# The low part of the gate-and-up weights: by an accumulating transfer instead of a VectorE subtraction

## The chip, the core and the metric

One core of one Trainium2 chip runs the whole program in one launch. The metric is device time in microseconds, as the median of the runs that were made. Engines are named as in the profile: PE is TensorE (matrix products), DVE is VectorE, ACT is ScalarE, POOL is GpSimd, SP is SyncE, which issues transfers.

## The reference, cut to what matters

Two layers of a decoder trunk on 512 tokens of 1024 features, all in float32: a token mixer, a cross-attention into 256 memory tokens, and a feed-forward part. Each has a norm before it and one behind it, and adds to the residual stream. The change touches the feed-forward part alone:

```python
def swiglu_ffn(h, w_gate_up, w_down):
    gate, up = jnp.split(h @ w_gate_up, 2, axis=-1)
    return (jax.nn.silu(gate) * up) @ w_down
```

`w_gate_up` is 1024 x 5632 per layer (twice 2816 columns), `w_down` 2816 x 1024.

## The kernel before

**Products from two parts.** TensorE multiplies faster in the type fp32r, which keeps fewer bits of a float32. Each operand is therefore split into a high part (the value rounded to fp32r) and a low part (value minus high part), and a product is three products, `mm3` (L204 to L211): high by high, high by low, low by high. In the trace these are lines L207, L208 and L209. `split` (L213) does it with two instructions: ScalarE copies the source into the high part, and VectorE subtracts the high part from the source.

**Weights in chunks.** A weight matrix goes through in chunks of 512 KB: a tile of 128 partitions by 1024 columns. `load` (L241) lets SyncE fetch a chunk into a raw tile (three buffers, L158); for the gate-and-up weights it consists of four row blocks of 256 columns, so its rows in DRAM are 1 KB long. `chunk` (L256) splits it into the tiles `hi` and `lo` (five buffers each, L159). `load` is called three chunks ahead of the one in use and `chunk` makes two ahead, but that is the order in which the code is written down. The order in which each engine runs its instructions is set by a scheduler at compile time, which places a split as soon as its buffers allow by its estimate. All engines run their queues in order.

**The feed-forward part** (`ffn`, L1176). The hidden columns are handled in two parts of 12 and 10 blocks of 128. For each pair of blocks there is a group, named `gu` in the profile, of two gate blocks and two up blocks: four chunks, first two for the gate, then two for the up columns. A chunk serves 24 products. Gate blocks are evacuated from PSUM by ScalarE (`silu`), up blocks by VectorE (`silu` times up), and the result is split again (`gh`, `gl`). Behind each part follow products with `w_down`, named `da` and `db`. There are 11 groups per layer, 44 chunks of `gu`, 88 in both layers.

**The start of the part.** The norm ahead of it (`prenorm`, L361, names with `ff`) runs in four token blocks of 128, here called blocks 0 to 3, while TensorE finishes the output projection of the cross-attention (`xo0b` in layer 0, `xo1b` in layer 1) and begins with the first `gu` group. That group runs its four chunks twice: first for tokens 0 to 255, then for 256 to 511, so that it can begin before blocks 2 and 3 are normalised. The chain of one block is: ScalarE squares the projection (`junk`), VectorE prepares `xo0p_t`, GpSimd takes the power -0.5 (`xo0p_r`, L228), VectorE updates the residual `h`, ScalarE squares that (`ff_hn`), VectorE prepares `ff_t`, GpSimd takes the power (`ff_r`), VectorE writes the normalised `ff_hn`, TensorE transposes it (`ff_pt`), and ScalarE and VectorE split the transpose into `hTff_h` and `hTff_l`. The transposes of blocks 2 and 3 stand in TensorE's queue among the products of the first `gu` group.

GpSimd does little else than these powers; all transfers are issued by SyncE.

Of the kernel before, what the change touches and what calls it, by code (L numbers as in the profile page):

```python
# [10 lines left out]
F32 = mybir.dt.float32  # L11
F32R = mybir.dt.float32r
# [14 lines left out]
# SBUF tiles of 2 KB, by stream: slots of a stream are given out in the order of emission  # L27
# [6 lines left out]
def shape_constants():  # L34
    """Identity, triangles, block and window masks, rotary frequencies: all from shapes alone."""
    c = np.zeros((128, C_END), np.float32)
    p = np.arange(128)[:, None]
    f = np.arange(128)[None, :]
    c[:, C_ID:C_ID + 128] = p == f
    c[:, C_U:C_U + 128] = p <= f  # L40
    c[:, C_LV:C_LV + 128] = (p // 64 == f // 64) & ((p // 32) % 2 == 1) & ((f // 32) % 2 == 0)
    for n, shift in enumerate((256, 256, 128, 0)):
        d = shift + p - f
        cnt = ((d >= 0) & (d <= 128)) * 1.0 + ((d >= 0) & (d % 4 == 0)) + ((d >= 0) & (d % 16 == 0))
        with np.errstate(divide="ignore"):
            m = np.where(cnt > 0, 8.0 * np.log(np.maximum(cnt, 1.0)), NEG)
        c[:, C_AM + n * 128:C_AM + (n + 1) * 128] = m
    c[:, C_M:C_M + 128] = p % 32 == f % 32
    half = np.arange(0, 16, 2, dtype=np.float32)
    c[:, C_IF:C_IF + 8] = (np.float32(500000.0) ** (-half / np.float32(16.0)))[None, :]  # L50
    return c


class Driver:
    """Interleaves the emission of dependent chains with bulk products on a running estimate of TensorE's time.

    A task is a generator; it yields how long its next step has to wait (ns), or the name of an event.
    """
# [11 lines left out]
    def lag(self, extra=0.0):  # L70
        """Until VectorE and ScalarE are through with what they have been given."""
        return max(max(self.engines.values()) - self.t, 0.0) + 300.0 + extra
# [37 lines left out]
class Engine:  # L110
    """An engine whose instructions are also counted on the driver's clock."""
# [14 lines left out]
class Group:  # L126
    """One projection: columns of a weight against activations, feature- or token-major."""
# [22 lines left out]
class Trunk:  # L150
# [44 lines left out]
    def mm(self, out, a, b, start=True, stop=True):  # L195
        """float32 product of up to 128 columns."""
        self.nc.tensor.matmul(out, a, b, start=start, stop=stop)  # L197
        self.dr.t += 215.0 * max(128, out.shape[-1]) / 128
# [5 lines left out]
    def mm3(self, out, wh, wl, xh, xl, first, last):  # L204
        """float32 product from parts of 12 bits: (wh + wl)^T (xh + xl)."""
        mm = self.nc.tensor.matmul
        mm(out, wh, xh, start=first, stop=False)  # L207
        mm(out, wh, xl, start=False, stop=False)  # L208
        mm(out, wl, xh, start=False, stop=last)  # L209
        self.dr.t += 3 * max(107.0, out.shape[-1] / 2.37)  # L210

# [6 lines left out]
    def rsqrt(self, name, a, add, eps, mul=None):  # L218
        """(a + add + eps)^-0.5 or (a * mul + eps)^-0.5, per element."""
        nc = self.nc  # L220
        w = a.shape[-1]
        t = self.sm(name + "_t", w)
        if mul is not None:
            self.v.tensor_scalar(t, a, mul, eps, op0=MUL, op1=ADD)
        else:
            self.v.tensor_scalar(t, a, add, eps, op0=ADD, op1=ADD)
        r = self.sm(name + "_r", w)
        nc.gpsimd.tensor_tensor(r, t, self.nhalf[:, :w], op=ALU.pow)  # L228
        return r

    def wbc(self, name, row, tag="e"):
        """A weight row on every partition, in two halves."""
        t = []
        for i in range(2):
            x = self.B(tag, name)
            self.nc.sync.dma_start(x, bass.AP(tensor=row.tensor, offset=row.offset + i * 512, ap=[[0, 128], [1, 512]]))
            t.append(x)
        return t

# [1 line left out]
    def load(self, upto):  # L241
        """Load and split weight chunks, in the order of their use."""
        nc = self.nc
        while len(self.loaded) <= upto and len(self.loaded) < len(self.order):
            g, (cols, ks) = self.order[len(self.loaded)]
            nk, width = len(ks), sum(n for _, n in cols)
            raw = self.raw_p.tile([128, 1024], F32, tag="raw", name=g.name + "_raw")
            rv = raw[:, :nk * width].rearrange("p (k n) -> p k n", k=nk)
            o = 0
            for c0, n in cols:  # L250
                src = g.w[ks[0] * 128:(ks[0] + nk) * 128, c0:c0 + n].rearrange("(k p) n -> p k n", p=128)
                nc.sync.dma_start(rv[:, :, o:o + n], src)
                o += n
            self.loaded.append((ks, raw, nk, width, g.name))

    def chunk(self, i):  # L256
        """(k tiles, hi, lo) of chunk i; the ones behind it are on their way."""
        self.load(i + self.AHEAD + 1)
        while len(self.made) <= min(i + self.AHEAD, len(self.order) - 1):
            ks, raw, nk, width, name = self.loaded[len(self.made)]  # L260
            hi = self.w_p.tile([128, 1024], F32R, tag="whi", name=name + "_hi")
            lo = self.w_p.tile([128, 1024], F32R, tag="wlo", name=name + "_lo")
            n = nk * width
            self.split(hi[:, :n], lo[:, :n], raw[:, :n])
            self.made.append((ks, hi[:, :n].rearrange("p (k n) -> p k n", k=nk),
                              lo[:, :n].rearrange("p (k n) -> p k n", k=nk)))
            self.loaded[len(self.made) - 1] = None
        return self.made[i]
# [81 lines left out]
    def transposed(self, name, src, dst_hi, dst_lo):  # L350
        """src: two [128 tok, 512]; (hi, lo) of its transpose for each group of 4 k tiles."""
        for kg in range(2):
# [4 lines left out]
            n = 4 // len(his)  # L357
# [31 lines left out]
    @staticmethod  # L389
    def tok_act(d):  # L390
        """Operands kept as one (hi, lo) pair of [128, tokens] per k tile."""
        return lambda k, tb: tuple(x[:, tb * 128:tb * 128 + 128] for x in d[k])

    def out_groups(self, name, w, act, rows, kts, after, tag):
        """Output projection, post-norm, residual add; after(tb) follows each block. rows: (post weights)."""
# [27 lines left out]
    def h_tiles(self, src, tbs=range(NTB)):  # L423
        """The residual stream from DRAM: per token block two tiles of 512 features."""
# [21 lines left out]
    def setup2(self):  # L446
# [27 lines left out]
        # zeroed scratch around the diagonal blocks  # L474
# [11 lines left out]
    @staticmethod  # L486
    def full(d, c):
        """The four heads' 128 x 128 matrices of a chunk in scratch."""
        return d[c * 4:c * 4 + 4, :128, :].rearrange("h i j -> i h j")

    @staticmethod
    def diag(d, i, j, n, m):
        """Of their 32 x 32 diagonal blocks, (chunk, head, block) in order, the n x m from row i and column j."""
        return bass.AP(tensor=d.tensor, offset=d.offset + i * 128 + j, ap=[[32 * 129, 64], [128, n], [1, m]])

    def rotary(self):
        """cos and sin of position * frequency, after an exact reduction by multiples of 2 pi."""
# [41 lines left out]
    def mixer(self, l, box, y):  # L539
        """Groups of the input projection; the chains behind them are spawned as their inputs appear."""  # L540
# [17 lines left out]
        def conv_silu(pre, tag, n0, store, after):  # L558
            """2 * silu of the causal depthwise convolution, feature-major."""
# [13 lines left out]
        def sumsq(pre, xs, res):  # L573
            """Per-token 1 / norm of each head: [128 tok, (chunk, head)]."""
# [10 lines left out]
            # the four partial sums of a token lie 32 partitions apart  # L585
# [24 lines left out]
        def gates():  # L610
# [8 lines left out]
            # softplus(a) = max(a, 0) + log1p(exp(-|a|)), log1p(e) = 2 artanh(e / (2 + e))  # L619
# [26 lines left out]
        def gdn_front():  # L646
# [12 lines left out]
            # the same by rows, on all partitions  # L659
# [24 lines left out]
            for c in range(NTB):  # L684
# [4 lines left out]
                # exp(-|decay_i - decay_j|): below the diagonal the decay from j to i, above it from i to j  # L689
# [24 lines left out]
            # 32 x 32 diagonal blocks, half of the columns of one per partition: forward substitution  # L714
# [32 lines left out]
            for pair in ((0, 1), (2, 3)):  # L747
# [6 lines left out]
                # blocks of 64 and 128  # L754
# [11 lines left out]
                for c in pair:  # L766
# [4 lines left out]
                    # of X only the first block is needed on  # L771
# [38 lines left out]
        def queries():  # L810
# [5 lines left out]
            # the doubled silu and the doubled values take a quarter  # L816
# [172 lines left out]
        def pair_attention(pr):  # L989
            qk, vtok = st["qk"], st["vtok"]  # L990
            y[pr] = (self.B("a", f"yTh{pr}", dt=F32R), self.B("a", f"yTl{pr}", dt=F32R))
            for tb in range(NTB):
                n = (tb + 1) * 128
                Ps = []
                for s in range(2):
# [5 lines left out]
                    # minus the masked scores, and minus their maximum  # L1001
# [44 lines left out]
    def memory(self, l, mT, event):  # L1046
        """Normalised memory, transposed and split."""
# [177 lines left out]
    def run(self):  # L1225
# [14 lines left out]
        for l in range(2):  # L1240
# [3 lines left out]
            def chain_norm(name, event, row, box, tag="e", spill=False):  # L1244
                """after(tb) of an output projection: the next sub-layer's norm."""
# [86 lines left out]
```

## Time and profile before

| | |
|---|---|
| median of 3 runs | 1660.26 us (1658.7 to 1662.85) |
| span of the profiled execution | 1660.5 us |
| transfers, whole span | 174.56 MB, mean 105 GB/s, all issued by SyncE, 34.6% of the time of 16 DMA engines |
| loads of `gu_raw` | 88 of 512 KB |
| first and last `gu_lo` | 446.0 and 1572.1 us from the start of the span |

For the profiled execution the profile gives its span, which is 0.24 us above the median of the runs. Times in the timeline are microseconds from the start of the span. A row of the timeline has the start, the duration, the engine, the line, the operation, output and inputs with their shapes, and in square brackets how long the engine had been idle before it and what ended that. The line is often a helper's: L122 is the wrapper through which all VectorE and ScalarE instructions go, so instructions are told apart by the names of their tiles. A row of the grouped view ends with the total busy time, the mean duration in ns, and the idle time before the group with what ended most of it. A row of the view of waits has the total, the number of waits and the longest. A row of the view by stretches has the stretch and its length, then busy time and count of PE, weight loads, DVE, ACT and POOL, the granted clock of TensorE, the busy share of the DMA engines, and GB/s.

### The profile page before, as it was taken

To read this page: it belongs to the slowest core of one execution; us is meant where nothing else is said; L and a number is where in the kernel's file an instruction comes from. 1 tells how busy PE (TensorE), PEld (TensorE's weight loads), DVE (VectorE), ACT (ScalarE), POOL (GpSimd) and SP (SyncE) were. 2 spreads that over 40 slices of the span, in tenths; PEclk is the share of its full clock that TensorE was granted. 3 is DMA by queue.
4 is the path that set the end of the run, shared out by engine and by line. 5 is a ranking of instruction groups with operands and counts; after the bars stand their busy time and mean duration, and the time that the engine had idled before them with its cause. 6 is when DMAs were issued, how large, how long until landed. Compare 5 with 4: busy or idle time off the path is not lost.

```text
span 1660.5 us, 21539 instructions
## 1 busy us (share of the span) xinstructions
PE 1619.2 (98%) x8457; PEld 1361.5 (82%) x8457; DVE 878.8 (53%) x1640; ACT 644.3 (39%) x1195; POOL 73.4 (4%) x76
## 2 busy tenths in 40 slices
PE   7999999999999999999999999999999999999998
PEld 6878777888888888888788778778888888888886
DVE  6979475745463332233489785667455533223334
ACT  5543344544343222332345443455344423223221
POOL 0010000100010000000000200000000100000000
PEclk9999999999999999999999999999999999999999
DMA  6445323442233323334333351425421332333331
GB/s 189 134 125 117 94 88 128 137 155 65 75 91 101 100 91 102 98 93 127 89 106 112 95 146 58 133 70 165 140 76 52 114 102 89 101 93 97 102 101 51
DMA packets 169201, 174.56 MB, mean 105 GB/s; under 512 B 29950, under 2 KB 132620, under 8 KB 169100
## 3 DMA queue, kind: packets, MB, share of 16 engines
q1 hardware_dynamic: 169100, 173.19, 34.6%
q8 instruction: 66, 1.08, 0.3%
q14 instruction: 35, 0.29, 0.1%
HBM read 163.71 MB, written 9.45 MB: 104 GB/s over the span
## 4 chain that ended last, share of the span: by engine, by line
PE 77%; DVE 11%; issue 3%; DMA 3%; POOL 3%; ACT 3%; SPq 0%; POOLq 0%; DVEq 0%; ACTq 0%
DVE h L122 1%; PE yp L197 1%; PE sc L197 1%; DMA Z<-dZ 1%; PE dZ L197 1%; PE O L197 1%; DMA edrow<-dD 1%; DVE gq_c L122 1%; PE W1p L197 1%; DVE X L122 1%; DVE xk_lo L122 1%; ACT junk L122 1%; DVE t L122 0%; POOL ff_r L228 0%; DVE xa_hn L122 0%
## 5 line engine op out<-in xcount | busy, mean ns | idle before, releaser
L122 DVE TENSOR_TENSOR gu_lo<-gu_raw,gu_hi 128x1024 fp32r<-128x1024 f32 x88 | 107.7, 1224 | 260.8 <-ACT gu_hi L122 260.8
L122 ACT ACTIVATE gu_hi<-gu_raw 128x1024 fp32r<-128x1024 f32 x88 | 93.1, 1060 | 228.4 <-issue 109.9
L122 DVE TENSOR_TENSOR da_lo<-da_raw,da_hi 128x1024 fp32r<-128x1024 f32 x24 | 29.4, 1225 | 83.1 <-ACT da_hi L122 83.1
L122 DVE TENSOR_TENSOR db_lo<-db_raw,db_hi 128x1024 fp32r<-128x1024 f32 x20 | 24.5, 1225 | 58.0 <-ACT db_hi L122 58.0
L122 ACT ACTIVATE da_hi<-da_raw 128x1024 fp32r<-128x1024 f32 x24 | 25.5, 1060 | 74.9 <-issue 23.7
L122 ACT ACTIVATE gh<-silu 128x512 fp32r<-128x512 f32 x44 | 27.2, 622 | 51.6 <-DVE silu L122 51.6
L122 ACT ACTIVATE db_hi<-db_raw 128x1024 fp32r<-128x1024 f32 x20 | 21.2, 1060 | 58.6 <-issue 23.7
L122 DVE TENSOR_TENSOR gl<-silu,gh 128x512 fp32r<-128x512 f32 x44 | 30.1, 688 | 14.2 <-ACT gh L122 14.2
L228 POOL TENSOR_TENSOR ffnp_r<-ffnp_t,nhalf 128x1 f32<-128x1 f32 x8 | 4.4, 548 | 707.3 <-DVE ffnp_t L122 707.3
L122 DVE TENSOR_TENSOR xq_lo<-xq_raw,xq_hi 128x1024 fp32r<-128x1024 f32 x16 | 19.6, 1226 | 24.3 <-ACT xq_hi L122 23.8
L122 ACT ACTIVATE P<-P,m 128x128 f32<-128x128 f32 (+3 forms) x32 | 17.9, 560 | 27.1 <-DVE m L122 25.8
L201 PE MATMUL mix_pt<-cst,mix_hn 128*128 128x128 f32 x64 | 13.1, 346 | 14.8 <-DVE mix_hn L122 13.3
L122 ACT ACTIVATE xq_hi<-xq_raw 128x1024 fp32r<-128x1024 f32 x16 | 17.0, 1061 | 23.9 <-DMA xq_raw<-in_w_xq 4.9
L122 DVE TENSOR_TENSOR xv_lo<-xv_raw,xv_hi 128x1024 fp32r<-128x1024 f32 x16 | 19.6, 1225 | 12.0 <-ACT xv_hi L122 11.5
L122 ACT ACTIVATE junk<-dacc 128x512 f32<-128x512 f32 x16 | 10.1, 629 | 39.4 <-DVE dacc L122 39.3
L122 ACT ACTIVATE xP<-xs,xm 128x256 f32<-128x256 f32 x32 | 14.9, 470 | 26.6 <-DVE xm L122 26.6
L201 PEld LDWEIGHTS mix_pt<-cst,mix_hn 128*128 128x128 f32 x64 | 9.0, 174 | 18.0 <-DVE mix_hn L122 12.0
L122 ACT ACTIVATE xk_hi<-xk_raw 128x1024 fp32r<-128x1024 f32 x16 | 16.9, 1057 | 14.3 <-DMA xk_raw<-in_w_xkv 13.0
L122 ACT ACTIVATE xv_hi<-xv_raw 128x1024 fp32r<-128x1024 f32 x16 | 17.0, 1060 | 14.1 <-DMA xv_raw<-in_w_xkv 4.8
L122 DVE TENSOR_TENSOR xk_lo<-xk_raw,xk_hi 128x1024 fp32r<-128x1024 f32 x16 | 19.3, 1216 | 3.7 <-ACT xk_hi L122 3.7
L197 PE MATMUL sc<-qkT,qkT 64*128 64x128 f32 (+3 forms) x64 | 20.6, 482 | 0.0
L122 DVE TENSOR_TENSOR X<-X,t 64x31 f32<-64x31 f32 (+30 forms) x62 | 19.3, 312 | 1.1
(2283 smaller groups left out, 5418.5 us busy)
## 6 DMA issues: line engine op xcount, KB each, us to landing
gu_raw<-in_w_gate_up SPq DMA_DIRECT2D x88, 512.0 KB, 3.5
da_raw<-in_w_down SPq DMA_DIRECT2D x24, 512.0 KB, 3.8
db_raw<-in_w_down SPq DMA_DIRECT2D x20, 512.0 KB, 3.8
xk_raw<-in_w_xkv SPq DMA_DIRECT2D x16, 512.0 KB, 3.6
xv_raw<-in_w_xkv SPq DMA_DIRECT2D x16, 512.0 KB, 4.6
xq_raw<-in_w_xq SPq DMA_DIRECT2D x16, 512.0 KB, 4.5
h<-in_x SPq DMA_DIRECT2D x16, 256.0 KB, 4.8
gk_raw<-in_w_in SPq DMA_DIRECT2D x8, 512.0 KB, 7.9
```

What stands on the lines that cost most here:

```text
L122: return f(*args, **kw)
L197: self.nc.tensor.matmul(out, a, b, start=start, stop=stop)
L201: self.nc.tensor.transpose(out, src, self.ident)
L228: nc.gpsimd.tensor_tensor(r, t, self.nhalf[:, :w], op=ALU.pow)
```

## The change

In `chunk`, chunks whose group's name begins with `gu` take another way. ScalarE writes the high part as before, and then a second copy, the negated high part, into `lo`. Then GpSimd issues a transfer that adds the raw tile onto `lo` (both in SBUF), which leaves raw minus high. All other chunks are split as before. The rest of the difference is comments and docstrings that are left out.

```diff
             hi = self.w_p.tile([128, 1024], F32R, tag="whi", name=name + "_hi")
-            lo = self.w_p.tile([128, 1024], F32R, tag="wlo", name=name + "_lo")
             n = nk * width
-            self.split(hi[:, :n], lo[:, :n], raw[:, :n])
+            if name.startswith("gu"):
+                lo = self.w_p.tile([128, 1024], F32R, tag="wlo", name=name + "_lo")
+                self.a.activation(hi, raw, AF.Copy)
+                self.a.activation(lo, hi.bitcast(F32), AF.Copy, scale=-1.0)
+                self.nc.gpsimd.dma_start(lo.bitcast(F32), raw, accum_op=ADD)
+            else:
+                lo = self.w_p.tile([128, 1024], F32R, tag="wlo", name=name + "_lo")
+                self.split(hi[:, :n], lo[:, :n], raw[:, :n])
```

How it moves instructions at the start of the feed-forward part of layer 0. On ScalarE, around the split of the second chunk (number 1, tiles `gu0_raw_4345` before and after) and the work for blocks 1 and 2; before:

```order
L122 ACTIVATE junk_80,xo0_sq_4288<-xo0b_2__4431 128x512
L122 ACTIVATE gu0_hi_4359<-gu0_raw_4345 128x1024
L122 ACTIVATE hTff_h0_4382<-ff_pt_4497 128x4x128
L122 ACTIVATE hTff_h1_4383<-ff_pt_4504 128x4x128
L122 ACTIVATE ff_hn_4511,ff_ss_4513<-h_2533 128x512
L122 ACTIVATE ff_hn_4512,ff_ss_4513<-h_2535 128x512
```

and after:

```order
L122 ACTIVATE junk_80,xo0_sq_4288<-xo0b_2__4433 128x512
L122 ACTIVATE gu0_hi_4360<-gu0_raw_4345 128x1024
L122 ACTIVATE hTff_h0_4384<-ff_pt_4499 128x4x128
L122 ACTIVATE gu0_lo_4361<-gu0_hi_4360 128x1024
L122 ACTIVATE hTff_h1_4385<-ff_pt_4506 128x4x128
L122 ACTIVATE ff_hn_4513,ff_ss_4515<-h_2533 128x512
L122 ACTIVATE ff_hn_4514,ff_ss_4515<-h_2535 128x512
```

The negating copy of chunk 1 stands between the two copies of block 1's transpose. A little later on the same engine, the splits of chunks 2, 3 and 4 and the squares of block 3 (`h_2537` and `h_2539`); before:

```order
L122 ACTIVATE gu0_hi_4562<-gu0_raw_4357 128x1024
L122 ACTIVATE gu0_hi_4608<-gu0_raw_4560 128x1024
L122 ACTIVATE junk_80,xo0_sq_4317<-xo0b_3__4490 128x512
L122 ACTIVATE gu0_hi_4652<-gu0_raw_4606 128x1024
L122 ACTIVATE hTff_h0_4382<-ff_pt_4579 128x4x128
L122 ACTIVATE hTff_h1_4383<-ff_pt_4586 128x4x128
L122 ACTIVATE ff_hn_4549,ff_ss_4551<-h_2537 128x512
```

and after:

```order
L122 ACTIVATE gu0_hi_4564<-gu0_raw_4358 128x1024
L122 ACTIVATE junk_80,xo0_sq_4317<-xo0b_3__4492 128x512
L122 ACTIVATE gu0_lo_4565<-gu0_hi_4564 128x1024
L122 ACTIVATE gu0_hi_4611<-gu0_raw_4562 128x1024
L122 ACTIVATE hTff_h0_4384<-ff_pt_4582 128x4x128
L122 ACTIVATE hTff_h1_4385<-ff_pt_4589 128x4x128
L122 ACTIVATE gu0_lo_4612<-gu0_hi_4611 128x1024
L122 ACTIVATE gu0_hi_4656<-gu0_raw_4609 128x1024
L122 ACTIVATE ff_hn_4551,ff_ss_4553<-h_2537 128x512
```

The split of chunk 4 (`gu0_hi_4656`) has moved from ahead of block 2's `hTff_h` to right ahead of block 3's squares, and two negating copies have come in. On GpSimd, the queue from the power of block 0 on, as a piece of the difference (a plus marks a row that only the changed kernel has):

```order
 L228 TENSOR_TENSOR ff_r<-ff_t,nhalf 128x1
 L228 TENSOR_TENSOR xo0p_r<-xo0p_t,nhalf 128x1
+L267 DMA gu_lo<-gu_raw 128x1024
 L228 TENSOR_TENSOR ff_r<-ff_t,nhalf 128x1
+L267 DMA gu_lo<-gu_raw 128x1024
 L228 TENSOR_TENSOR xo0p_r<-xo0p_t,nhalf 128x1
+L267 DMA gu_lo<-gu_raw 128x1024
 L228 TENSOR_TENSOR ff_r<-ff_t,nhalf 128x1
+L267 DMA gu_lo<-gu_raw 128x1024 x40
```

The transfers of chunks 1, 2 and 3 stand between the powers of blocks 2 and 3, and 40 more follow in one row up to the end of the layer's `gu` groups. On TensorE, where block 3 is transposed among the products of the first group; before:

```order
L207 MATMUL gu_2__4656<-hTff_h_4382,gu_hi 128x256
L208 MATMUL gu_2__4656<-hTff_l_4384,gu_hi 128x256
L209 MATMUL gu_2__4656<-hTff_h_4382,gu_lo 128x256
L207 MATMUL gu_3__4669<-hTff_h_4382,gu_hi 128x256
L208 MATMUL gu_3__4669<-hTff_l_4384,gu_hi 128x256
L201 MATMUL ff_pt<-cst,ff_hn 128x128 x4
L209 MATMUL gu_3__4669<-hTff_h_4382,gu_lo 128x256
```

and after:

```order
L207 MATMUL gu_2__4661<-hTff_h_4384,gu_hi 128x256
L201 MATMUL ff_pt<-cst,ff_hn 128x128 x4
L208 MATMUL gu_2__4661<-hTff_l_4386,gu_hi 128x256
L209 MATMUL gu_2__4661<-hTff_h_4384,gu_lo 128x256
L201 MATMUL ff_pt<-cst,ff_hn 128x128 x4
L207 MATMUL gu_3__4674<-hTff_h_4384,gu_hi 128x256
```

The first four transposes of block 3 have moved ahead of four products. SyncE's queue has the same loads in the same order; a load of a `gu` chunk into a raw tile that held a `gu` chunk now waits for the transfer that reads that tile, not for VectorE.

## Prediction

> **What bounds the kernel now.** I read the busy shares of the page first, then who makes TensorE wait, then the stretches in which the changed weights are used, and last the timeline where TensorE does wait.
>
> ```profile
> PE 1619.2 (98%) x8457; PEld 1361.5 (82%) x8457; DVE 878.8 (53%) x1640; ACT 644.3 (39%) x1195; POOL 73.4 (4%) x76
> ```
>
> TensorE (PE) is busy in 98% of the span; VectorE (DVE), which the change relieves, in 53%. So nothing can come back but the 41 us in which TensorE is idle, and of those only what VectorE causes near the gate-and-up products. The busy times of two stretches inside the feed-forward part of layer 0 and TensorE's waits in it:
>
> ```profile
> 494.40:647.00 152.60, 152.60 (x675) 126.38 (x674) 49.55 (x51) 44.39 (x55) 0.00 (x0) 1.00 0.33 101
> 654.00:760.00 106.00, 106.00 (x469) 87.82 (x468) 34.47 (x36) 31.38 (x39) 0.00 (x0) 1.00 0.32 97
> ```
>
> ```profile
> PE ff_pt L201 <- DVE ff_hn L122: 4.4, 4, 1.5
> ```
>
> The first number behind the stretch is its length, the second TensorE's busy time: they are equal, so from 494.4 us on TensorE never waits there, at a granted clock of 1.00, with the DMA engines busy a third of the time (0.33, 101 GB/s). Its only waits near the gate-and-up products are these four, 4.4 us in both layers together: for the normalised blocks 2 and 3 (`ff_hn`), whose transposes stand inside the first gate-and-up group. That is 0.26% of the span and the most that the change can give.
>
> **The change part by part.** What is removed and what takes its place on ScalarE (ACT):
>
> ```profile
> L122 DVE TENSOR_TENSOR gu_lo<-gu_raw,gu_hi 128x1024 fp32r<-128x1024 f32 x88 | 107.7, 1224 | 260.8 <-ACT gu_hi L122 260.8
> L122 ACT ACTIVATE gu_hi<-gu_raw 128x1024 fp32r<-128x1024 f32 x88 | 93.1, 1060 | 228.4 <-issue 109.9
> ```
>
> VectorE loses 88 x 1.224 = 107.7 us. ScalarE gains a second copy of the same shape, 88 x 1.06 = 93 us: in the first stretch above, with 28 chunks' worth of time (5.44 us each, below) and at most one extra copy in each, its busy time goes from 44 to about 74 of 152.6 us, so it does not become the bound. GpSimd (POOL) gets 88 issues, and the 16 DMA engines 88 accumulating transfers of 512 KB. All these hide under TensorE if the low part arrives before its product. How early the chunks are split, in steady state:
>
> ```profile
> 499.66 1.06 ACT L122 ACTIVATE gu_hi<-gu_raw 128x1024 fp32r<-128x1024 f32 x1 [3.26 <-issue]
> ...
> 505.10 1.06 ACT L122 ACTIVATE gu_hi<-gu_raw 128x1024 fp32r<-128x1024 f32 x1 [1.94 <-PE gu__4841 L208]
> ...
> 510.54 1.06 ACT L122 ACTIVATE gu_hi<-gu_raw 128x1024 fp32r<-128x1024 f32 x1 [3.89 <-issue]
> ```
>
> A chunk lasts 5.44 us, and a split waits for the product that frees a slot, five chunks before its own. It is needed four chunks later, after 21.8 us. Two copies take 2.1 us, so the transfer may take up to 19 us in the single case. Call x the time from the end of the negating copy until the sum has landed. The raw tile is now held until then, and there are three: copies 2.12, x, and the reload (3.66, below) must fit into 3 x 5.44 = 16.3 us, so x may be 10.5. Behind a split that waits for its raw tile stand on ScalarE the silu copies that empty PSUM; they have about one chunk of slack.
>
> No accumulating transfer and no GpSimd issue is in the trace. The nearest rows, 512 KB each, median us from issue to landing last:
>
> ```profile
> gu_raw<-in_w_gate_up SPq DMA_DIRECT2D x88, 512.0 KB, 3.5
> ...
> gk_raw<-in_w_in SPq DMA_DIRECT2D x8, 512.0 KB, 7.9
> ```
>
> The lower end of x is a plain load, 3.5; the upper end the load beside crowded queues, 7.9. I take 6: a load occupies 0.33 x 5.44 = 1.8 us of all 16 engines; the accumulation reads two sources, so 3.5 + 1.8 = 5.3, and 0.7 for the issue by GpSimd (a 128x1 operation takes it 0.55, below). That is an estimate, nearer to the lower row because the transfer has one neighbour, not many. [...] No run shown here has such a transfer.
>
> What is left is the start of each feed-forward part, where there is no lead of four chunks. ScalarE, VectorE, GpSimd and TensorE there in layer 0:
>
> ```profile
> 461.67 1.06 ACT L122 ACTIVATE gu_hi<-gu_raw 128x1024 fp32r<-128x1024 f32 x1 [0.62 <-PE xo0b__4490 L209]
> 462.64 1.07 ACT L122 ACTIVATE hTff_h<-ff_pt 128x512 fp32r<-128x512 f32 x2
> ...
> 469.44 1.06 ACT L122 ACTIVATE gu_hi<-gu_raw 128x1024 fp32r<-128x1024 f32 x1 [1.57 <-DMA gu_raw<-in_w_gate_up]
> 470.40 1.09 ACT L122 ACTIVATE hTff_h<-ff_pt 128x512 fp32r<-128x512 f32 x2
> 473.16 0.63 ACT L122 ACTIVATE ff_hn<-h 128x512 f32<-128x512 f32 x1 [1.67 <-DVE h L122]
> ```
>
> ```profile
> 464.56 1.22 DVE L122 TENSOR_TENSOR gu_lo<-gu_raw,gu_hi 128x1024 fp32r<-128x1024 f32 x1
> ...
> 475.02 1.22 DVE L122 TENSOR_TENSOR gu_lo<-gu_raw,gu_hi 128x1024 fp32r<-128x1024 f32 x1
> 476.68 1.41 DVE L122 SCALAR_TENSOR_TENSOR ff_hn<-h,ff_r,w_ff 128x512 f32<-128x512 f32 x2 [0.44 <-POOL ff_r L228]
> ```
>
> ```profile
> 459.77 0.55 POOL L228 TENSOR_TENSOR ff_r<-ff_t,nhalf 128x1 f32<-128x1 f32 x1 [3.03 <-DVE ff_t L122]
> ...
> 475.25 1.40 POOL L228 TENSOR_TENSOR ff_r<-ff_t,nhalf 128x1 f32<-128x1 f32 x1 [2.91 <-DVE ff_t L122]
> ```
>
> ```profile
> 469.56 1.29 PE L201 MATMUL ff_pt<-cst,ff_hn 128*128 128x128 f32 x8 [1.49 <-DVE ff_hn L122]
> ...
> 476.20 0.28 PE L208 MATMUL gu__4656<-hTff_l,gu_hi 128*128 128x256 f32 x1
> 476.32 0.28 PE L209 MATMUL gu__4656<-hTff_h,gu_lo 128*128 128x256 f32 x1
> ...
> 477.58 0.63 PE L201 MATMUL ff_pt<-cst,ff_hn 128*128 128x128 f32 x4 [0.74 <-DVE ff_hn L122]
> ```
>
> *Gained.* GpSimd's power operation took 1.40 us at 475.25, beside VectorE's `gu_lo`, and 0.55 without it. With `gu_lo` gone, block 2's `ff_hn` comes about 1.3 us earlier, for which TensorE waited 1.49; and block 3's chain from the square on ScalarE (473.16) to the transpose (477.58), 4.42 us, shrinks by 0.85 to 3.57.
>
> *Lost.* The raw tile of chunk 4 is chunk 1's. Chunk 1's low part ended at 464.56 + 1.22 = 465.78, and the split of chunk 4, waiting for the load, started at 469.44: 3.66 us for the reload. After the change chunk 1's high part ends at 462.73, one `hTff_h` (half of 1.07) follows, then the negating copy, to 464.32 (the order shown with the change has these rows); the sum lands at 464.32 + x, chunk 4's raw at 467.98 + x, its split ends at 469.04 + x. In ScalarE's order block 3's squares stand right behind that split, as they did before, when it was early enough to cost nothing. With x = 6 they start at 475.04, not 473.16: 1.88 later. With the chain 0.85 shorter, the transpose is at 478.61, 1.03 later. TensorE now has it four products earlier in its order, so 4 x 0.12 = 0.48 us more work is behind it: 1.51 us later in all. The gain at block 2 is swallowed, since TensorE only waits longer here. Chunks 1 and 2 are cut close too: the sum of chunk 2 lands around 475.4, when TensorE is about there; that wait ends before the one at block 3, so it adds nothing.
>
> Per layer that is x - 4.49, not below -0.23 (where ScalarE's copies, no longer the load, hold the squares). GpSimd's in-order queue now has a transfer ahead of block 3's two power operations; their negating copies end by 469 and 472, before those operations' inputs, so this costs nothing unless one issue takes over a microsecond. SyncE (SP) issues the same loads in the same order; behind a load that waits stand only further weight loads. Layer 1 has the same pattern:
>
> ```profile
> 1290.64 1.06 ACT L122 ACTIVATE gu_hi<-gu_raw 128x1024 fp32r<-128x1024 f32 x1 [1.65 <-DMA gu_raw<-in_w_gate_up]
> ```
>
> So the sum is 2 x 1.51 = +3.0 us, with -0.5 at x = 3.5 and +6.8 at x = 7.9. The profiled span of 1660.5 us is 0.2 above the median of the three runs (1660.26), so the sum is made on the median: 1663.3.
>
> **The rivals.** *The start is held longer.* The same place, with x of 7 to 10.5, because GpSimd's issue is slow or because load and accumulation share the engines: +5 to +12 us, 1665 to 1672. It counts as slower from x = 7 on, since 0.3%, about what a measurement can tell from no change, is 5 us. For it: the 7.9 of `gk_raw`. Against: the DMA engines are a third busy here.
>
> *The transfers become the bound.* Each chunk needs its load (1.8 us of 16 engines) and its accumulation within 5.44 us. A second copy's worth makes 3.6, two copies' worth 5.4, which just fits; from 2.1 copies' worth on the DMA engines set the pace. At three it is 7.2 us a chunk, 1.8 more; over the 80 or so chunks behind the starts +140, about 1800 us. For it: the arithmetic of the adder is nowhere in the trace. Against: its rows are four times as long as those of the loads, so two copies' worth should be less than 3.6. [...]
>
> *Faster.* The wait at block 3 also goes, if chunk 4's raw tile is there in time and the squares go with VectorE's earlier `h`: at most the 4.4 us of idle time, 1656. Against: the floor of -0.23 per layer from ScalarE's own copies.
>
> *It does not do what it says*: the scheduler still places a VectorE subtraction. The order shows none, so no chance is given.
>
> **How the numbers follow.** Forecast, hidden in steady state with x between 3.5 and 7: 0.57, 1659.8 to 1665.3. Start held longer: 0.21. Transfers the bound: 0.18. Faster: 0.04, of which about half beyond 0.3%, if something unseen adds to it. The range takes the first two and the spread of the runs (1658.7 to 1662.85, some 2 us to either side), 1656 to 1676, and leaves out the third. Faster 0.02, same 0.59, slower 0.39.
>
> **What would show it.** Right: TensorE without waits from the second gate-and-up group on; `gu_lo` landing 5 to 7 us after its issue; the wait for `ff_pt` at block 2 gone and at block 3 grown from 0.74 to some 3.6 us; chunk 4's split waiting for its load until about 474 on that layer's clock; power operations at 0.55. Wrong: TensorE waiting for `gu_lo` by DMA in the middle of the feed-forward part, a DMA share near 1 there, ScalarE waiting for `gu_raw` at every chunk, or GpSimd's issues taking microseconds.

## The result, and the profile after

The changed kernel takes 1676.19 us (median of 4 runs, 1672.97 to 1680.06), beside 1661.55 us (4 runs, 1658.7 to 1664.13) for the kernel before on the same chip: ratio 1.0091, 95% interval 1.0078 to 1.0105. It is slower by 0.9%, where 1663.3 us, no measurable change, was forecast. The profiled execution took 1676.67 us, its span is 1674.6 us, 14.1 more than before.

The page, busy shares and the new queue:

```profile
PE 1624.1 (97%) x8457; PEld 1366.8 (82%) x8457; DVE 773.3 (46%) x1552; ACT 730.9 (44%) x1283; POOL 144.7 (9%) x164
...
q0 software_dynamic: 12672, 46.14, 15.5%
...
gu_raw<-in_w_gate_up SPq DMA_DIRECT2D x88, 512.0 KB, 4.7
...
gu_lo<-gu_raw POOLq DMA_DIRECT2D x88, 512.0 KB, 5.7
```

VectorE lost 105.5 us and ScalarE gained 86.6, close to the 107.7 and 93 worked out. The sum lands 5.7 us (median) after its issue. In a queue's row stand packets, MB and the share of 16 engines: 15.5% of 1674.6 us over 88 transfers is 2.95 us of all 16 engines each, more than a load's 1.8. And the loads of `gu_raw` now take 4.7 us instead of 3.5.

TensorE's waits near the gate-and-up products:

```profile
PE ff_pt L201 <- DVE ff_hn L122: 6.1, 2, 3.5
...
PE gu__4916 L207 <- ACT silu L122: 2.4, 1, 2.4
...
PE gu__11484 L209 <- DMA gu_lo<-gu_raw: 1.8, 1, 1.8
PE gu__4661 L209 <- DMA gu_lo<-gu_raw: 1.7, 1, 1.7
```

These are 12.0 us instead of 4.4. Where they lie, by stretches: first the changed kernel, then two comparable stretches of the kernel before.

```profile
467.00:500.00 33.00, 27.78 (x212) 27.18 (x211) 8.46 (x15) 18.18 (x26) 6.10 (x8) 0.90 0.62 144
...
500.00:520.00 20.00, 17.64 (x71) 14.17 (x70) 1.98 (x3) 7.87 (x10) 3.44 (x4) 0.91 0.89 209
...
520.00:600.00 80.00, 80.00 (x354) 66.22 (x354) 13.43 (x18) 37.50 (x43) 11.17 (x13) 1.00 0.88 197
...
1294.00:1328.40 34.40, 30.02 (x215) 29.21 (x214) 9.06 (x16) 18.87 (x28) 6.09 (x8) 0.85 0.63 142
```

```profile
466.00:494.40 28.40, 26.14 (x212) 25.36 (x211) 16.43 (x24) 12.13 (x20) 4.19 (x3) 1.00 0.36 110
1287.00:1315.00 28.00, 25.75 (x210) 24.99 (x209) 16.05 (x23) 12.14 (x19) 4.19 (x3) 1.00 0.35 107
```

From 520 to 600 us TensorE never waits (80.00 of 80.00, clock 1.00): the steady state holds, though the DMA engines are now busy 0.88 of the time, where 0.30 to 0.33 was enough before. The loss is in the two starts (467 to 500 and 1294 to 1328) and in the 20 us behind the first. It has two halves: idle time, and a granted clock of 0.85 to 0.91.

*Idle time.* ScalarE, and the reload on SyncE, at the start in layer 0:

```profile
464.00 1.05 ACT L122 ACTIVATE gu_lo<-gu_hi 128x1024 fp32r<-128x1024 f32 x1
...
471.02 1.08 ACT L122 ACTIVATE gu_lo<-gu_hi 128x1024 fp32r<-128x1024 f32 x1
476.75 1.06 ACT L122 ACTIVATE gu_hi<-gu_raw 128x1024 fp32r<-128x1024 f32 x1 [4.65 <-DMA gu_raw<-in_w_gate_up]
477.72 0.61 ACT L122 ACTIVATE ff_hn<-h 128x512 f32<-128x512 f32 x1
```

```profile
470.01 0.37 SPq L252 DMA_DIRECT2D gu_raw<-in_w_gate_up  x1
```

Chunk 1's negating copy ends at 465.05, and SyncE issues the reload of its raw tile at 470.01, when the sum is there: x = 4.96. The reload then lasts until chunk 4's split at 476.75: 6.74 us, not 3.66. (In layer 1 the same two times are 4.91 and 6.69.) Block 3's squares follow at 477.72, and TensorE waits for its transpose:

```profile
480.93 1.09 PE L201 MATMUL ff_pt<-cst,ff_hn 128*128 128x128 f32 x4 [3.54 <-DVE ff_hn L122]
```

*The clock.* Stretches of 2 us behind that wait in layer 0, behind the wait for `silu`, and in layer 1; the figure before the last two is the granted clock with the DMA share behind it:

```profile
478.00:480.00 2.00, 0.00 (x0) 0.00 (x0) 0.21 (x1) 1.98 (x5) 0.56 (x1) 0.55 0.81 265
480.00:482.00 2.00, 1.07 (x5) 1.10 (x6) 1.41 (x2) 0.00 (x0) 0.89 (x1) 0.50 0.76 237
482.00:484.00 2.00, 2.00 (x12) 2.00 (x11) 0.73 (x2) 1.19 (x2) 0.00 (x0) 0.50 1.11 229
484.00:486.00 2.00, 2.00 (x15) 2.00 (x15) 0.66 (x1) 0.00 (x0) 0.00 (x0) 0.74 0.42 78
486.00:488.00 2.00, 2.00 (x19) 2.00 (x18) 0.00 (x0) 0.00 (x0) 0.00 (x0) 1.00 0.27 81
...
516.00:518.00 2.00, 2.00 (x5) 1.63 (x6) 0.00 (x0) 2.00 (x3) 0.55 (x1) 0.50 0.51 98
518.00:520.00 2.00, 2.00 (x8) 1.58 (x7) 0.00 (x0) 0.26 (x1) 0.86 (x1) 0.71 0.93 174
```

```profile
1304.00:1306.00 2.00, 1.94 (x8) 1.65 (x8) 0.00 (x0) 1.66 (x4) 0.00 (x0) 0.56 1.00 196
...
1308.00:1310.00 2.00, 1.48 (x7) 1.51 (x8) 1.03 (x2) 0.36 (x1) 0.76 (x1) 0.50 0.93 266
1310.00:1312.00 2.00, 2.00 (x12) 2.00 (x11) 1.14 (x2) 0.84 (x2) 0.00 (x0) 0.50 1.09 214
1312.00:1314.00 2.00, 2.00 (x11) 2.00 (x11) 0.25 (x1) 0.00 (x0) 0.00 (x0) 0.50 0.27 51
1314.00:1316.00 2.00, 2.00 (x17) 2.00 (x17) 0.00 (x0) 0.00 (x0) 0.00 (x0) 0.88 0.13 26
```

A stretch that is busy throughout holds 11 products at clock 0.50 (1312 to 1314) and 19 of the same size at 1.00 (486 to 488). So a busy TensorE hides a loss here, which the table puts at busy time times (1 - clock). That is a little high, since 11 products are more than half of 19.

| | more idle than before | lost to the clock |
|---|---|---|
| start, layer 0 | 5.22 - 2.26 = 3.0 | 1.07 x 0.50 + 2 x 0.50 + 2 x 0.26 = 2.1 |
| wait for `silu`, layer 0 | 20.00 - 17.64 = 2.4 | 2 x 0.50 + 2 x 0.29 = 1.6 |
| start, layer 1 | 4.38 - 2.25 = 2.1 | 1.94 x 0.44 + 1.48 x 0.50 + 4 x 0.50 + 2 x 0.12 = 3.8 |

The sum is 15.0, for 14.1 us more span. A count that does not need the clock is how much later TensorE starts the product of the same number in its queue than in the kernel before: over these three stretches the delay grows by 4.7, 4.2 and 5.4 us, 14.3 in all. Less the 7.5 us of idle time, that leaves 6.8 for the clock: a little under half of the loss.

### The profile page after: what moved, and what is told of

The parts are those of the page before. It is cut to its first block, busy times and chain, and to the rows that moved or that the text cites. A ratio compares the mean times of both kernels' runs of the same rounds, so it can differ in the third digit from the quotient of the medians.

```text
span 1674.6 us, 21790 instructions
## 1 busy us (share of the span) xinstructions
PE 1624.1 (97%) x8457; PEld 1366.8 (82%) x8457; DVE 773.3 (46%) x1552; ACT 730.9 (44%) x1283; POOL 144.7 (9%) x164
## 3 DMA queue, kind: packets, MB, share of 16 engines
q0 software_dynamic: 12672, 46.14, 15.5%
## 5 line engine op out<-in xcount | busy, mean ns | idle before, releaser
L267 POOL DMA_DIRECT2D gu_lo<-gu_raw x88 | 76.2, 866 | 774.4 <-ACT gu_lo L122 772.6
L122 ACT ACTIVATE gu_lo<-gu_hi 128x1024 fp32r<-128x1024 f32 x88 | 92.9, 1056 | 1.6
L228 POOL TENSOR_TENSOR so_r<-so_t,nhalf 128x4 f32<-128x4 f32 x8 | 8.1, 1008 | 215.8 <-DVE so_t L122 215.8
L122 ACT ACTIVATE xk_hi<-xk_raw 128x1024 fp32r<-128x1024 f32 x16 | 16.9, 1058 | 14.1 <-DMA xk_raw<-in_w_xkv 12.9
```

The costliest lines, as they stand in the source:

```text
L122: return f(*args, **kw)
L267: self.nc.gpsimd.dma_start(lo.bitcast(F32), raw, accum_op=ADD)
```

## The experiments

Theory A, formed on this profile: everything is lost at the starts, because the raw tile is held until its sum has landed and because its reload runs beside other accumulations; block 3's norm, queued on ScalarE behind the split that waits for it, then makes TensorE wait, and the clock doubles the price. Rivals: B, the crowded DMA engines cost time in the steady state; C, ScalarE's extra copies are the cause; D, the accumulation costs time whatever the buffers. Unless another number is given, the kernel before took 1660.49 us (25 runs) beside the first four runs, 1660.99 (25 runs) beside the next four, and 1661.87 (12 runs) beside the last four. In the diffs, `j` counts a layer's gate-and-up chunks from 0.

**Where: all but the starts, and the starts alone.**

```diff
-            if name.startswith("gu"):
+            if name.startswith("gu") and j >= 8:
```

> The first eight gate-and-up chunks of each layer (two groups) are split as before, the other 72 by the accumulating transfer. If the loss sits at the start of each feed-forward part (the splits wait for raw tiles that the transfers hold, the squares of block 3 wait behind one such split, TensorE idles and its granted clock falls to 0.50): 1658 to 1664 us, no wait of TensorE on gu_lo, ff_pt waits of 4 to 5 us in all as before. If the loss is spread over all chunks (ScalarE's second copy, shared DMA engines): 72 of 88 parts of the 14 us stay, about 1672.

```diff
-            if name.startswith("gu"):
+            if name.startswith("gu") and j < 4:
```

> Only the first four chunks of each layer (the first group) use the accumulating transfer. If the loss sits at the start: the two starts cost 4.7 and 5.4 us in the profiled run of the changed kernel, so +9 to +11, 1670 to 1673; the wait for silu later in layer 0 (2.4 us and its slow clock) is gone. If it is spread over all chunks: 8 of 88 parts of 14 us, +1.3, 1663.

With the first eight chunks split as before: 1661.38 us, ratio 1.0001 (0.9991 to 1.0011), and the four waits for `ff_pt` of 4.4 us as before. 72 accumulations in the steady state cost nothing that can be measured; B falls. With only the first four chunks of each layer accumulated: 1671.72 us, ratio 1.0069 (1.0054 to 1.0084). Eight of 88 transfers bring 11 of the loss of about 14.6 us. Its waits:

```profile
PE ff_pt L201 <- DVE ff_hn L122: 6.2, 2, 3.3
...
PE gu__11443 L209 <- DMA gu_lo<-gu_raw: 2.0, 1, 2.0
...
PE gu__4660 L209 <- DMA gu_lo<-gu_raw: 1.5, 1, 1.5
```

They are those of the changed kernel without the one for `silu`, which with its clock was 4.0 us above. That one is a follow-up: ScalarE stands in line for a raw tile with the silu copies behind it, which needs the accumulations that come after the first four.

**What: the copies, or the transfer.** The second copy on ScalarE stays, VectorE adds; there is no transfer.

```diff
-                self.nc.gpsimd.dma_start(lo.bitcast(F32), raw, accum_op=ADD)
+                self.v.tensor_tensor(lo, raw, lo.bitcast(F32), op=ADD)
```

> ScalarE still writes the negated copy, but VectorE adds the raw tile onto it; no transfer on GpSimd. If transfers and the raw tiles that they hold cause the loss: 1660 to 1665 us, the split of chunk 4 within 5 us of chunk 1's low part. If ScalarE's 88 extra copies cause it: most of the 14 us stays, 1671 to 1677.

1660.86 us, ratio 1.0007 (0.9994 to 1.0020). The copies cost nothing that can be measured; C falls.

**How: block 3's squares ahead of the waiting split.** The changed kernel with chunk 4's split queued behind block 3's squares on ScalarE (`sq` is kept from `prenorm`, and the code of that chunk is written one call later).

```diff
+                with self.tc.issue_after(self.sq.ins):
                     self.a.activation(hi, raw, AF.Copy)
```

> As the changed kernel, but on ScalarE the split of chunk 4 is queued behind the squares of block 3, not ahead of them; nothing else is altered by hand. If block 3's squares waiting behind that split make the long wait at ff_pt: that wait falls from 3.5 and 2.5 us to under 1 us, the granted clock does not fall to 0.50 there, and 7 to 10 us of the 14 come back, 1665 to 1669; the wait of 1.7 us for chunk 2's low part and the one for silu stay. If GpSimd's queue or ScalarE's copies hold the chain of block 3, the wait stays and so does 1675.

1662.00 us, ratio 1.0012 (1.0003 to 1.0021): some 13 of the 14.6 us are gone, more than the 1665 to 1669 expected, since TensorE's wait for `silu` went too. The reload is as late as ever, only nobody stands behind it any more:

```profile
476.90 1.06 ACT L122 ACTIVATE gu_hi<-gu_raw 128x1024 fp32r<-128x1024 f32 x1 [3.10 <-DMA gu_raw<-in_w_gate_up]
```

No wait for `ff_pt` is left, in layer 0 the clock is 1.00 from 464 to 520 us, and the two waits for `gu_lo` (1.5 and 1.9 us) stand in place of the 4.4 us of before. The one of 1.9 us in layer 1 was still followed by half clock, so that the mean over the 10 us around it is 0.83; the interval of the ratio stays just above 1:

```profile
1290.00:1300.00 10.00, 8.06 (x55) 7.85 (x55) 4.71 (x8) 5.04 (x9) 2.33 (x3) 0.83 0.92 223
```

**The clock by itself.** Extra products, which nothing reads, fill TensorE's wait at block 3's transposes: first 24, then 52 per start.

```diff
+        if name == "ff" and tb == 3:
+            dummy = self.ps("a", "dummy", (128, 256))
+            for _ in range(24):
+                self.nc.tensor.matmul(dummy, hT[0][0][:, 0, 0:128], hT[0][0][:, 0, 0:256], start=True, stop=True)
```

> The changed kernel, with 24 extra products of 256 columns on TensorE, into a PSUM tile that nothing reads, right ahead of block 3's transposes. They leave the late reload as it is, and only keep TensorE busy while it waits there. Theory (a large part of the loss is the granted clock, which falls to half for some 6 us after TensorE has waited): the clock stays near 1.00 between 467 and 500 us and again at the start of layer 1, the wait of 3.5 us at ff_pt becomes nearly nothing, and the kernel is faster than the changed one although it does 48 products more: 1668 to 1673. Rival (the clock is a side effect and the wait alone costs): 48 products of 0.11 us fit into the two waits of 3.5 us, so 1675 to 1678, as the changed kernel, with the same clock rows.

1679.18 us, ratio 1.0113 (1.0081 to 1.0145), above both ranges that were expected, and inconclusive: in layer 0 the products were over at 477.04, 3.58 us of idle time were left behind them, and the clock still fell to 0.56. The scheduler also put block 3's transposes ten products earlier, which is 10 x 0.12 = 1.2 us more to wait for.

> As the run with 24 extra products, with 52 of them per start, 6.2 us of work in place of the whole wait, since 24 were over before block 3's norm was there and left 3.6 us of idle time. Theory (part of the loss is the half clock behind the wait): no idle time ahead of the transposes, clock 1.00 throughout 474 to 490, and the stretch up to 494 us ends some 2 us earlier than in the changed kernel, per layer: 1669 to 1674. Rival (the clock row is a by-product and work behind the wait is no slower for it): 1675 to 1679.

1673.24 us, ratio 1.0068 (1.0051 to 1.0085). The idle time ahead of the transposes is nearly gone in layer 0 (0.28 us), and the clock is 1.00 in every stretch from 474 to 486:

```profile
475.03 6.40 PE L384 MATMUL dummy<-hTff_h 128*128 128x256 f32 x52
481.71 1.29 PE L201 MATMUL ff_pt<-cst,ff_hn 128*128 128x128 f32 x8 [0.28 <-DVE ff_hn L122]
```

12 us of useless products do not make the kernel slower, and perhaps 3 us faster: the intervals of the ratios (1.0068 and 1.0091) overlap a little. The profiled execution, the slowest of the six (1677.91 us), does not show the 2 us per layer that were expected. Counted from product to product, layer 0's start costs 4.1 us there, against 4.7 in the changed kernel; the earlier transposes cost 1.2 of that, so some 1.8 us came back with the clock, near the table's 2.1. In layer 1 the start costs 5.4 us in both: the reload took 7.92 us there instead of 6.69, and 1.55 us of idle time were left. So the run agrees with a price for the clock in layer 0, and does not prove its size.

**The buffer.** A fourth raw tile; room comes from a scratch tile in bf16 and a setup tile that borrows a slot.

```diff
-        self.raw_p = pool("raw", 3)
+        self.raw_p = pool("raw", 4)
...
-        self.junk = self.cp.tile([128, 512], F32, name="junk")
+        self.junk = self.cp.tile([128, 512], mybir.dt.bfloat16, name="junk")
...
-        rows = self.cp.tile([128, 128], F32, name="rows")
+        rows = self.B("r", "rows", (128, 128))
```

> The changed kernel with four raw tiles instead of three (room is made by a smaller scratch tile, and by one setup tile in another pool); the same transfers, accumulations and engine orders. Theory (the loss is the raw tile that is held until its sum has landed, and a reload that is slow beside accumulations): chunk 4's raw tile no longer depends on chunk 1's sum, so block 3's squares start on time, the wait at ff_pt is back to about 1 us or gone, ScalarE's wait ahead of the silu copy is gone, and the clock stays at 1.00; the two waits for gu_lo of 1.7 us stay: 1660 to 1665. Rival (the transfers themselves, their contention with other work on the DMA engines or on SBUF's ports, cost the time whatever the buffers): 1672 to 1677.

> The kernel before with four raw tiles, made by the same two edits as in the changed kernel with four raw tiles (1655.0 us). It tells how much of those 5.9 us under the kernel before is the change, and how much the buffer. If the gain is the buffer's alone (earlier loads at several places of the program, where the changed kernel with four was already 3 to 9 us ahead of before outside the feed-forward parts), it comes to 1654 to 1657; VectorE's subtraction still delays block 2, so ff_pt waits of 1 to 4 us remain. If the change has a part in it, it stays at 1658 to 1661.

The changed kernel with four: 1655.04 us, ratio 0.9965 (0.9955 to 0.9976), below the range expected and the fastest of the study. All transfers are as they were, so D falls: with one more tile the same 88 accumulations run in 21 us less, of which some 5 come with the tile even without the change, as the next run shows. The kernel before with four: 1656.65 us, ratio 0.9967 (0.9955 to 0.9980). So the change itself is worth nothing measurable there; it trades one set of waits for another. With the change:

```profile
PE gu__11484 L209 <- DMA gu_lo<-gu_raw: 2.0, 1, 2.0
PE gu__4661 L209 <- DMA gu_lo<-gu_raw: 1.6, 1, 1.6
```

and without it:

```profile
PE ff_pt L201 <- DVE ff_hn L122: 4.4, 4, 1.5
```

What both gain lies outside the feed-forward part: among others the waits of the products `xk` in the cross-attention for `Kl`, 3.4 us in the kernel before, are in neither list of waits any more. The scratch tile in bf16 is no cause of it: a square into `junk` takes 0.60 us before and after.

**Adding, or only moving.** The transfer without the addition: the low part is then the raw value, and the products are those of other numbers.

```diff
-                self.nc.gpsimd.dma_start(lo.bitcast(F32), raw, accum_op=ADD)
+                self.nc.gpsimd.dma_start(lo.bitcast(F32), raw)
```

> The changed kernel with the transfer on GpSimd's queue a plain copy of the raw tile, without the addition: the low part is then the raw value, not raw minus high. Transfers, queue and order are otherwise the same. It tells the cost of adding (the destination is read as well) from that of a 512 KB transfer within SBUF issued by GpSimd. If the adding makes the transfers slow, gu_lo lands in about 4 us instead of 5.7, the DMA share of its queue falls well below 15.5%, the reload of chunk 4 takes 5 us instead of 6.7, and the time falls to 1663 to 1670. If it is the transfer and its queue, all of these stay and the time is 1674 to 1678.

1661.44 us, ratio 1.000 (0.999 to 1.001), below the lower end expected. The same bytes on the same queue:

```profile
q0 software_dynamic: 12672, 46.14, 7.0%
...
gu_raw<-in_w_gate_up SPq DMA_DIRECT2D x88, 512.0 KB, 3.6
...
gu_lo<-gu_raw POOLq DMA_DIRECT2D x88, 512.0 KB, 2.9
```

The addition doubles a transfer: 2.9 to 5.7 us until it has landed, 7.0% to 15.5% of the engines' time, and it is what slows the loads from 3.6 to 4.7.

**The reload without neighbours.** Only chunks 0 and 1 accumulate; block 3's squares are kept behind chunk 4's split.

```diff
-            if name.startswith("gu"):
+            if name.startswith("gu") and j in (0, 1):
```

> Only chunks 0 and 1 of each layer are made by accumulating transfers, all others by VectorE, with block 3's squares kept behind chunk 4's split. Chunk 1's sum still holds the raw tile of chunk 4, but no accumulation runs while that tile is loaded again. Theory (the reload took 6.7 us because the accumulations of chunks 2 and 3 ran beside it): SyncE issues the reload about 5 us after the end of chunk 1's negating copy, as in the changed kernel, and chunk 4's split starts 3.6 to 4.5 us after that. Rival (a load into a tile that an accumulation has just read is slow by itself, or the issue is late): 6 us or more. The scheduler places block 3's transposes later here, so the total says little: 1660 to 1664.

Chunk 1's negating copy and chunk 4's split on ScalarE, and the reload's issue:

```profile
463.88 1.05 ACT L122 ACTIVATE gu_lo<-gu_hi 128x1024 fp32r<-128x1024 f32 x1
...
473.39 1.06 ACT L122 ACTIVATE gu_hi<-gu_raw 128x1024 fp32r<-128x1024 f32 x1 [2.93 <-DMA gu_raw<-in_w_gate_up]
```

```profile
469.88 6.23 SPq L252 DMA_DIRECT2D gu_raw<-in_w_gate_up  x4
```

x is 469.88 - 464.93 = 4.95, as in the changed kernel, and the reload takes 473.39 - 469.88 = 3.51 us instead of 6.74. So the accumulations of chunks 2 and 3 beside it cost 3.2 us. (A single run, 1658.43 us, below the total expected; no wait for `ff_pt` is left, since block 3's transposes stand some 26 products later here.)

**Two candidates that brought nothing.** The squares first, and chunk 2 split by VectorE; and four raw tiles with the first three chunks split by VectorE.

```diff
-            if name.startswith("gu"):
+            if name.startswith("gu") and not (self.cnt[name] == 3):
```

> A candidate for better than both: the changed kernel with chunk 4's split queued behind block 3's squares on ScalarE (as in the run before), and chunk 2 of each layer, whose sum came too late for its product, split by VectorE as before the change. Expected: no wait at ff_pt, none or under 1 us for gu_lo at chunk 2, clock at 1.00 at both starts; the 4.4 us of waits for ff_pt in the kernel before are gone too, so 1656 to 1660 against 1660.5, ratio 0.9975 to 1.000. If VectorE's subtraction delays block 2's normalisation again (as in the kernel before), ff_pt waits of 1.5 us per layer come back and it is 1660 to 1662, the same as before.

1665.97 us, ratio 1.0022 (1.0011 to 1.0034): slower than forecast. The waits for `gu_lo` went, but TensorE waited for block 3's norm again (`ff_pt` 3.6 us in two waits), since the scheduler put the transposes 10 products earlier than in the changed kernel. ScalarE's line for raw tiles and the `silu` wait behind it came back (3.0 us), and a single wait of 1.96 us was enough for the clock:

```profile
474.00:476.00 2.00, 0.99 (x7) 0.93 (x8) 1.42 (x2) 0.92 (x2) 0.97 (x2) 0.92 0.93 203
476.00:478.00 2.00, 2.00 (x11) 2.00 (x10) 1.27 (x2) 0.87 (x2) 0.00 (x0) 0.50 0.95 194
```

```diff
-            if name.startswith("gu"):
+            if name.startswith("gu") and j >= 3:
```

(with the three edits for four raw tiles)

> A candidate: the changed kernel with four raw tiles, in which the first three chunks of each layer are split by VectorE as before the change. The waits of 1.6 and 2.0 us for chunk 2's sum should go; if nothing takes their place, 1651 to 1654 against 1655.0 with four raw tiles alone. If VectorE's subtractions hold up block 2's norm as in the kernel before, ff_pt waits of 1 to 3 us come back and it is 1654 to 1658.

1657.03 us, ratio 0.9971 (0.9960 to 0.9982): not distinguishable from four raw tiles alone. The `gu_lo` waits went, and 3.0 us of `ff_pt` waits came in their place.

## Why the prediction was wrong, point by point

- **Steady state hidden: right.** TensorE does not wait from 520 us on. But the margin is thinner than the forecast's case had it: 1.8 us of load and 2.95 of accumulation in 5.44 us per chunk. The rival in which transfers become the bound needed 5.4 us and got 4.75. Its sum took for granted that loads and accumulations share the engines; the loads agree with that, 3.5 us before and 4.7 beside the accumulations.
- **Gain at block 2 and shorter chain: right.** The wait at block 2 is gone; block 3's chain from the square (477.72) to the transpose (480.93) is 3.21 us, where 3.57 was expected. Nothing was won by it, as said.
- **x = 6: near, and on the safe side.** It was 4.96.
- **"3.66 for the reload": the step that failed.** This term of the sum was too small. It was read from a start in which no accumulation ran. The change itself puts the accumulations of chunks 2 and 3 beside that load, and it took 6.74 us; without them it takes 3.51. With both measured values the sum for one start is 4.96 + 6.74 - 3.66 - 4.49 = +3.55, where the idle time grew by 3.0 in layer 0. In layer 1 it is +3.45 by the same sum, and the idle time grew by 2.1, because TensorE already ran at half clock there before the transposes. So the form of the sum was right, and with the measured terms it gives +7.0 us, some 1667; the other half of the loss lies in what the sum left out, the clock and the wait for `silu`. The rival in which the start is held longer named this contention ("because load and accumulation share the engines"), but I looked for it in x, and argued it away with a DMA share of a third that was measured without the change.
- **Missing from the sum: the clock.** An idle TensorE was priced at its idle time. Behind the longer waits it worked at half clock for 3 to 8 us, about 7 us of loss in all. At the starts of the kernel before the clock was 1.00 throughout, behind waits of up to 1.5 us, so nothing there showed it. With this and the wait for `silu` the time passes even the rival with the start held longer (1665 to 1672).
- **"About one chunk of slack" for the silu copies: wrong in the first groups.** ScalarE stood 7.87 us for a raw tile, and TensorE 2.4 us for the copy behind it:

```profile
513.25 1.06 ACT L122 ACTIVATE gu_hi<-gu_raw 128x1024 fp32r<-128x1024 f32 x1 [7.87 <-DMA gu_raw<-in_w_gate_up]
```

  With block 3's squares ahead of the split (1662.00 us) or with a fourth tile (1655.04 us) TensorE does not wait there. That it is the late start, carried on through three raw tiles at a DMA share of 0.89, is likely but not shown: in the first candidate, where the squares stood ahead too, ScalarE again stood 8.0 us for a raw tile and TensorE 3.0 us for `silu`.
- **Chunk 2's sum "adds nothing": right for the idle time of the changed kernel**, where its 1.7 and 1.8 us lie ahead of the wait for block 3. For the clock it was not nothing: in layer 1 the clock fell right behind it. And it became the next wait as soon as the longer one went.
- **The sign "grown from 0.74 to some 3.6 us" at block 3: met by luck.** The wait was 3.54 us in layer 0, but the forecast had it as the whole idle time of the start; with the 1.68 us ahead of it TensorE idled 5.22 us. In layer 1 it was 2.54.

## What to carry to other kernels

When a step goes from an engine to a transfer, write down which buffer the transfer now holds, until when, and who is queued behind the next use of that buffer, and price the reload with the change's own traffic beside it. Look first where the pipeline has no lead: here 8 of 88 transfers made three quarters of the loss. Price a wait of TensorE together with the clock behind it: here it fell to 0.50 behind single waits of 1.84, 1.94 and 1.96 us, and behind 1.68 us with 0.8 us more in the same 3.41 us, but not behind a wait of 1.97 us nor one of 3.0. Move independent work (here a norm's squares) ahead of an instruction that can wait for a transfer before adding or giving up anything else.

## What the runs showed of the hardware

- **An accumulating transfer within SBUF** of 512 KB took 2.95 us of all 16 DMA engines in the changed kernel and landed after 5.7 us (median); a plain copy of the same shape on the same queue took 7.0% of 1659.6 us over 88, 1.32 us, and landed after 2.9. GpSimd was busy longer with its issue too, 0.87 us (76.2 us for 88) against 0.54 (47.1 for 88):

```profile
L267 POOL DMA_DIRECT2D gu_lo<-gu_raw x88 | 76.2, 866 | 774.4 <-ACT gu_lo L122 772.6 <-PE ff_pt L201 1.8
```

- **A product in fp32r beside one in float32.** In the kernel before, 16 float32 products of 128 columns took 1.95 us, 0.12 each; with 52 extra products in the changed kernel, those, in fp32r and of 256 columns, took 6.40 us, 0.12 each as well (the row is with that run). The type is that of the kernel's tiles; the rows have f32 for both.

```profile
186.92 1.95 PE L197 MATMUL W1p<-Z,Q 128*128 128x128 f32 x16
```

- **The clock fell behind some waits of about 2 us, and not behind others.** It halved after single waits of 1.84 us (changed kernel, layer 1), 1.94 us (squares first, layer 1) and 1.96 us (the first candidate), not after one of 1.97 us (four raw tiles, layer 1), nor after the 3.0 us for `silu` in the first candidate, nor after those of 1.5 us in the kernel before. What told them apart is how a wait lay on a grid. Up to the last products of the program, every stretch at half clock in the 14 traces lasted 3.41 us, or twice or three times that, and within a trace all of them began on one grid of 3.41 us. First the three grid steps ahead of the drops in the changed kernel, then the two across which the 1.97 us lie with four raw tiles:

```profile
474.79:478.20 3.41, 1.22 (x8) 1.02 (x8) 0.00 (x0) 1.45 (x2) 0.00 (x0) 1.00 1.05 239
512.33:515.74 3.41, 1.24 (x6) 0.70 (x4) 0.00 (x0) 2.46 (x3) 0.05 (x1) 1.00 0.91 296
1300.81:1304.22 3.41, 1.57 (x13) 1.37 (x12) 0.20 (x1) 0.00 (x0) 0.17 (x1) 1.00 1.06 238
```

```profile
1283.53:1286.94 3.41, 2.33 (x20) 2.13 (x18) 1.68 (x4) 3.05 (x6) 1.51 (x3) 1.00 1.06 244
1286.94:1290.36 3.42, 2.52 (x21) 2.52 (x22) 1.30 (x3) 0.75 (x2) 0.82 (x1) 1.00 1.08 222
```

  TensorE was busy 0.36, 0.36 and 0.46 of the steps ahead of a drop, and 0.68 and 0.74 of the two without one. Over the 14 traces the clock fell after every step at full clock that was busy less than 0.44 (53 of them), and after none that was busy more than 0.50; between the two it went either way (5 fell, 5 did not). So two short waits in one step did what one long wait did: in layer 0 the drop at 478.20 comes 0.8 us into the wait of 3.54 us, with the 1.68 us for chunk 2's sum in the same step.

  TensorE worked again from 480.93 us on in layer 0, and the clock was whole at about 485 us (0.50 from 482 to 484 us, 0.74 from 484 to 486, 1.00 from 486 on).
